# The second gate computed in the first gate's tile during the MLP, rings of five weight tiles, and a new table of order and engines

## The chip, the cores and the metric

The kernel runs on one core of a Trainium2 chip. The metric is device microseconds for one execution; the number for a kernel is the median of its runs. The engines are PE (matrix products), DVE (vector), ACT (scalar functions), POOL (GpSimd) and SP, which here only issues DMA transfers.

## The reference

One layer over 512 tokens of width 1024, one batch, all in fp32:

```
sh1, sc1, gt1, sh2, sc2, gt2 = split(silu(c) @ w_ada + b_ada, 6)
h = rms_norm(x) * (1 + sc1) + sh1
q, k, v, iq, ik, iw, ca, cg = split(h @ w_in)
attn = sparse attention: indexer scores (iq, ik, iw), top 128 keys a query
       (causal by chunks of 64), softmax over these, 8 heads of 64
conv = silu(layer_norm(depthwise conv of 31 taps (ca * sigmoid(cg))))
x = x + gt1 * (concat(rms_norm(attn), rms_norm(conv)) @ w_out)
h2 = rms_norm(x) * (1 + sc2) + sh2
out = x + gt2 * (relu(h2 @ w_ff1)^2 @ w_ff2)          # D_FF = 4096
```

`c` is one row of 1024, so each of the six parts of the first line is one row of 1024 that depends on no token. `gt1` scales the output projection, `gt2` the MLP's result at the very end.

## The kernel before

Every fp32 product is made of three products of split operands: a value is kept as a rounded part `hi` and a rest `lo = x - hi`, and `mm3` multiplies hi·hi, hi·lo and lo·hi into one PSUM bank. Weights are loaded raw (`wr_`, 512 KB a load), cast to `wh_` on ACT and subtracted to `wl_` on DVE or POOL (`split_now`, line 857). `wh_` and `wl_` come from rings of four tiles of 128x512 each: a fifth split waits until the first tile's last matmul has read it.

No engine's order is written out by hand. The code records every operation (`_Plan`, line 211), and `schedule` (line 308) walks through a model of the engines and starts, on each free engine, the ready operation of the lowest level. The levels come from the table `URG`, the engine of an operation that could run on several comes from `ENG` (P is POOL, V is DVE, A is ACT, T is PE), and `POOL_TAPS` says how many of the 31 convolution taps of each of four feature groups run on POOL. Where an entry of `ENG` has four letters, they stand for the four weight tiles of a group of loads or for the four parts of a matrix in turn. `issue` (line 402) then emits all instructions in that order from one line, so every row of the trace carries L436; tiles are told apart by name.

In order of time: loads and `ada` products (the six parts of the first line), input projections (`c`, `iq`, `q`, `k`, `v`), convolution taps (`run` on DVE, `cacc` on POOL), index scores and top-k (`m`, `sc`: eight maxima a step, MAX8 and MATCH_REPLACE8), attention for tokens 0 to 255 (`pS` scores, `sl` softmax, `pP` transposes, `pO`), the output projection (`oA` and `oC` into `x`), attention for tokens 256 to 511 (with `oB`), and the MLP. The MLP works through four blocks of 1024 of D_FF: block 0 for the first 256 tokens (`fA`, `yA`), blocks 1 to 3 for all 512 tokens (`fF`, then `ff2_seven`, line 1595), block 0 for the last 256 tokens (`fB`, `yB`). `ff2_seven` makes the second product from seven products of sums of quarters (p1, p7, p2, p6, p4, p5, p3, of 24 matmuls each) where the plain way would need eight: `t1F` and `qF` are sums of weight quarters, `fF` sums of activations, `wl_p1F` and so on the rests of those sums, `llp1F` the rests of activations, and `facc` and `uF` collect the results out of PSUM.

The two gates: `gt1` is computed on PE (`ps_gt`, then spread to all partitions). `gt2` is computed by `add_gemv_vector` (line 782): eight loads of 512 KB rows of `w_ada`, one multiplication and seven multiply-adds of 128x1024 on DVE into the tile, then the sum over partitions as two products with a matrix of ones (`pg_gt`) and two additions of the bias. Both gates have a tile of 128x1024 of their own; gt2 is recorded ahead of the MLP's first operation, with a level that puts it early in the program. It is first read in the last block (`finish`, line 1581).

Of the kernel before, what the change touches and what calls it, by code (L numbers as in the profile page):

```python
# [11 lines left out]
F32 = mybir.dt.float32  # L12
F32R = mybir.dt.float32r
# [17 lines left out]
NEG_MASK = -1.0e30  # L31
FILLER = False
URG = dict(
    ahead_c1=1128.32, ahead_iq=281.4, warm=-938.21, g0=-145.45, gr=-855.15, w72=-213.15, ps72=247.73,
    start=-1053.53, glu=-116.74, c0=-592.48, ik=-123.04, iq=-263.01, iqn=762.72, idx=-479.26, rel=-170.37,
    topk=183.27, c1=788.58, q=79.07, qn=394.99, k=113.44, kn=-88.5, qT=190.86, v=212.78, vn=-145.05, kT=-114.04,
    tapV0=3.46, tapV1=-1171.22, tapV2=354.3, tapV3=88.85, tapP0=89.85, tapP1=1138.33, tapP2=-785.21,
    tapP3=-939.21, sh2=46.69, sc2=777.66, gt1=-370.45, gt2=-144.05, gemv_step=20.799999999999997,
    ahead_x=550.67, ahead=102.55, cn=128.0, pyc=-1037.03, oC=476.28, attn=-1036.57, sm=-332.0999999999998,
    pv=-4.8000000000000345, sq=-97.20000000000007, oA=402.92, n2=50.33, ff=639.29, tapVs=27.400000000000006,  # L40
    tapPs=81.65000000000006, topks=9.050000000000011, idxs=12.400000000000002, ns=22.250000000000007,
    projs=6.549999999999992, cns=33.55000000000003, oCs=9.299999999999999, evict=403.92, usum=28.34,
    attns=33.15000000000006, topkB=1515.0, qTB=381.12, attnB=201.26, oB=693.93, n2B=653.09,
)
ENG = dict(
    sl0B="P", sl1B="V", oAmul0="P", oAmul1="P", oAadd0="P", oAadd1="P", oBmul0="P", oBmul1="P", oBadd0="V",
    oBadd1="V", gt1="T", gt2="V", round0="T", round1="T", round2="T", round3="T", sl0="A", sl1="P", rope_q="P",
    rope_k="P", rope_iq="P", gb="P", oAadd="P", oCmul="A", oAmul="V", lo_c0="V", lo_c1="V", lo_iq="P", lo_q="P",
    lo_k="P", lo_v="P", lo_oC="P", lo_oA="P", lo_oB="P", lo_f1A="PPVP", lo_f2A="PVPV", lo_f1F="PVVP",
    lo_f2F="VVPP", lo_f1B="VVVV", lo_f2B="VVVP", sumF="VPVV", losF="VVVV", fsumF="V", fhiF="A", floF="V",  # L50
    uaddF="V", foldF="V", frest="V", h2lo0="V", h2lo1="V", aff0="A", aff1="A", mixA="P", tap0="A",
)
POOL_TAPS = (7, 5, 11, 12)
NB = 4
NA = 1
NBLK = 16
# [460 lines left out]
def layer_kernel(  # L517
# [24 lines left out]
    pl = _Plan(tc)  # L542
# [27 lines left out]
    def blk(shape, dt, name):  # L570
        return big.tile(shape, dt, tag="B", bufs=NBLK, name=name)
# [9 lines left out]
    def wk_bank(name):  # L581
        return pwk.tile([P, 512], F32, tag="wk", name=name)
# [4 lines left out]
    def raw(ap):  # L587
        return ap.bitcast(F32)
# [125 lines left out]
    sh2 = const.tile([P, KD], F32, name="sh2")  # L714
# [136 lines left out]
    def split_weights(src, name, lo_eng, place=None):  # L851
        with pl.urgency(pl.level[0] - URG.get("ahead_" + name[:2], URG["ahead"])):
            return split_now(src, name, lo_eng, place)

    def split_now(src, name, lo_eng, place):
        r = wts.tile([P, 2, 512], F32, tag="raw", name=f"wr_{name}", fifo=True)
        if len(src.shape) == 4:
            for j in range(2):
                pl.sync.dma_start(r[:, j, :].rearrange("p (s c) -> p s c", s=2), src[:, j])
        else:  # L860
            pl.sync.dma_start(r, src)
        res = []
# [175 lines left out]
    rope_q = Rope(g_q, "q", HD**-0.5)  # L1038
# [59 lines left out]
    for ct in range(4):  # L1098
# [13 lines left out]
    for i in range(1, NT):  # L1112
        n = (i + 1) * P
        sc[i] = const.tile([P, n], F32, name=f"sc{i}")
        for h in range(H):
            pl.level = (URG["idx"] + (8 * i - 8 + h) * URG["idxs"],)
            ps = wk_bank(f"pidx{i}_{h}")
            q = slice(i * P, (i + 1) * P)
# [3 lines left out]
            rel = ps  # L1122
# [65 lines left out]
    qT = []  # L1188
# [3 lines left out]
    kT = [blk([P, 4, S], F32R, f"kT{a}") for a in range(2)]  # L1192
# [12 lines left out]
    for t in range(NT):  # L1205
        v = banks[t].rearrange("p (h d) -> p h d", d=HD)
# [386 lines left out]
    def ff2_seven(b, part, f, lev_load, start):  # L1595
# [7 lines left out]
        with pl.after([start]), pl.urgency(lev_load):  # L1603
            for g, n in ((0, 0), (0, 1), (1, 1), (1, 0)):
                q = blk([P, 4, 512], F32, f"q{part}{b}{g}{n}")
# [126 lines left out]
    for part, blocks in PHASES:  # L1732
        for b in blocks:
            fts = []
            pair = blk([P, 2, 4, 256], F32, f"f{part}{b}") if part in SEVEN and part != "F" else None
            mark = len(pl.ops)
            for g in range(2):
                step += 1
                pl.level = (URG["ff"] + 20 * step,)
                fts.append(ff1(b, g, part, pair))  # L1740
            start = next(op for op in pl.ops[mark:] if op.engine == "tensor")
            if part in SEVEN:
                lev_load = pl.level[0] - 20
                step += 1
                pl.level = (URG["ff"] + 20 * step,)
                step += 1
                ff2_seven(b, part, fts, lev_load, start)
                for h in dict(A=(0,), B=(1,), F=(0, 1))[part]:
                    count[h] += 1
                continue  # L1750
            for n in range(2):
                step += 1
                pl.level = (URG["ff"] + 20 * step,)
                ff2(b, n, part, fts)
            for h in dict(A=(0,), B=(1,), F=(0, 1))[part]:
                count[h] += 1
# [53 lines left out]
```

## Time and profile before

| | |
|---|---|
| median of 3 runs | 648.05 us (646.64 to 649.21) |
| profiled execution | 649.53 us |
| its span, first to last instruction | 647.4 us |
| mean granted clock of PE | 0.993 |
| busy: PE, DVE, ACT, POOL | 624.2, 512.1, 368.1, 285.1 us |
| HBM read | 89.73 MB |

The span is 2.1 us shorter than the profiled execution: what lies around the first and last instruction isn't in the trace. A busy time counts the engine's own instructions; matmuls overlap, so a duration of 0.39 us for a matmul of 128x512 says less than the distance from one to the next. The stage table further down cuts the span into the stages named above.

### The profile page before, as it was taken

The page shows a single profiled execution, that of the slowest core. Times are in us where ns is not written, and L with a number is a line of the kernel's source. Part 1 is how long each engine was busy: PE and PEld are TensorE (multiplying, and loading weights), DVE is VectorE, ACT ScalarE, POOL GpSimd, SP SyncE. Part 2 cuts the span into 40 slices and gives each one's busy share as a digit, 9 for nine tenths or more (in the row PEclk, how much of TensorE's full clock was granted, in tenths as well). Part 3 has the DMA queues.
Part 4 walks back from the last instruction along what each step waited for, and adds up shares of the span by engine and source line. Part 5 has one row for each costly group of instructions (what it writes and reads, how often), then busy time and mean ns, then how long its engine had stood idle before and what let it go on. Part 6 is the DMA issues. An engine that isn't in the chain of part 4 may idle for free.

```text
span 647.4 us, 9888 instructions
## 1 busy us (share of the span) xinstructions
PE 624.2 (96%) x3390; PEld 500.7 (77%) x3390; DVE 512.1 (79%) x998; ACT 368.1 (57%) x745; POOL 285.1 (44%) x291
## 2 busy tenths in 40 slices
PE   4999999999999899999999999999999999999997
PEld 3766687778776677789878888878887888878985
DVE  4657999999999899997484638985389953699975
ACT  3326534985539853997375438744485435765552
POOL 3007915999999687637573611025110151100011
PEclk9999999999999799999999999999999999999999
DMA  9969997523120162144727830029310183100772
GB/s 291 348 200 399 382 334 243 201 80 98 33 76 24 33 222 73 33 136 126 227 67 251 302 97 2 1 62 336 108 48 1 42 316 98 32 2 2 221 219 79
DMA packets 56219, 94.55 MB, mean 146 GB/s; under 512 B 5913, under 2 KB 22505, under 8 KB 56170
## 3 DMA queue, kind: packets, MB, share of 16 engines
q1 hardware_dynamic: 56074, 93.91, 43.9%
q8 instruction: 26, 0.43, 0.3%
q14 instruction: 23, 0.19, 0.1%
q10 hardware_dynamic: 96, 0.03, 0.0%
HBM read 89.73 MB, written 2.10 MB: 142 GB/s over the span
## 4 chain that ended last, share of the span: by engine, by line
PE 62%; DVE 14%; POOL 7%; ACT 5%; SPq 4%; issue 4%; DMA 3%; ACTq 0%; DVEq 0%; POOLq 0%
PE fF L436 20%; SPq L436 4%; PE c L436 4%; PE fB L436 4%; PE yB L436 3%; PE oC L436 3%; PE yA L436 3%; PE fA L436 3%; PE iq L436 3%; PE p5F L436 3%; PE p1F L436 2%; DVE sc L436 2%; PE p4F L436 2%; PE p3F L436 2%; DVE run L436 2%
## 5 line engine op out<-in xcount | busy, mean ns | idle before, releaser
L436 PE MATMUL fF<-h,wh_fF 128*128 128x512 f32 x384 | 118.3, 389 | 0.0
L436 PEld LDWEIGHTS fF<-h,wh_fF 128*128 128x128 f32 x384 | 72.1, 188 | 15.0
L436 POOL TENSOR_TENSOR wl_fF<-wr_fF,wh_fF 128x512 fp32r<-128x512 f32 x24 | 36.1, 1523 | 103.5 <-ACT wh_fF L436 63.5
L436 PE MATMUL fF<-h,wl_fF 128*128 128x512 f32 x192 | 74.8, 390 | 0.2 <-POOL wl_fF L436 0.2
L436 ACT CAST wh_fF<-wr_fF 128x512 fp32r<-128x512 f32 x48 | 29.5, 622 | 60.3 <-PE fF L436 41.2
L436 DVE SCALAR_TENSOR_TENSOR run<-u,wdw,run 128x512 f32<-128x512 f32 x85 | 60.4, 745 | 0.2
L436 PEld LDWEIGHTS fF<-h,wl_fF 128*128 128x128 f32 x192 | 36.0, 188 | 8.0 <-POOL wl_fF L436 0.6
L436 POOL TENSOR_TENSOR cacc<-cacc,prod 128x512 f32<-128x512 f32 x31 | 40.0, 1292 | 4.7 <-ACT prod L436 3.4
L436 POOL TENSOR_TENSOR wl_yB<-wr_yB,wh_yB 128x512 fp32r<-128x512 f32 x4 | 5.1, 1288 | 69.6 <-ACT wh_yB L436 69.6
L436 ACT ACTIVATE fF<-fF 128x512 f32<-128x512 f32 x48 | 29.1, 613 | 7.2 <-PE fF L436 5.8
L436 DVE TENSOR_TENSOR wl_p1F<-qF,wh_p1F 128x512 fp32r<-128x512 f32 x12 | 8.3, 689 | 28.4 <-PE fF L436 28.4
L436 POOL TENSOR_TENSOR qF<-qF,qF 128x512 f32<-128x512 f32 x9 | 14.0, 1552 | 37.0 <-issue 22.0
L436 DVE TENSOR_TENSOR qF<-qF,qF 128x512 f32<-128x512 f32 x27 | 26.1, 992 | 1.4 <-DMA qF<-in_w_ff_dram 1.1
L436 POOL TENSOR_TENSOR wl_iq<-wr_iq,wh_iq 128x512 fp32r<-128x512 f32 x8 | 10.2, 1290 | 38.6 <-ACT wh_iq L436 38.6
L436 PE MATMUL c<-hTlo,wh_c 128*128 128x512 f32 x64 | 25.9, 405 | 0.2 <-DVE hTlo L436 0.2
L436 DVE TENSOR_TENSOR wl_fF<-wr_fF,wh_fF 128x512 fp32r<-128x512 f32 x24 | 16.7, 710 | 11.7 <-ACT wh_fF L436 11.4
L436 DVE MATCH_REPLACE8 sc<-m,sc 128x256 f32<-128x256 f32 (+2 forms) x48 | 25.7, 539 | 0.0
L436 PE MATMUL c<-hThi,wl_c 128*128 128x512 f32 x64 | 25.4, 397 | 0.0
L436 DVE MAX8 m<-sc 128x8 f32<-128x256 f32 (+2 forms) x48 | 25.1, 545 | 0.0
L436 PE MATMUL c<-hThi,wh_c 128*128 128x512 f32 x64 | 24.4, 401 | 0.7 <-ACT hThi L436 0.6
L436 ACT ACTIVATE prod<-u,wdw 128x512 f32<-128x512 f32 x31 | 21.9, 719 | 4.0 <-POOL cacc L436 3.9
L436 PE MATMUL fA<-h2a,wh_fA 128*128 128x256 f32 x128 | 23.9, 286 | 0.0
(394 smaller groups left out, 1972.7 us busy)
## 6 DMA issues: line engine op xcount, KB each, us to landing
wr_fF<-in_w_ff_dram SPq DMA_DIRECT2D x24, 512.0 KB, 3.8
qF<-in_w_ff_dram SPq DMA_DIRECT2D x24, 512.0 KB, 9.2
wa_gt<-in_w_ada_dram SPq DMA_DIRECT2D x16, 512.0 KB, 9.0
ada<-in_w_ada_dram SPq DMA_DIRECT2D x12, 512.0 KB, 8.7
wr_c<-in_w_in_dram SPq DMA_DIRECT2D x16, 256.0 KB, 7.6
wa_sh<-in_w_ada_dram SPq DMA_DIRECT2D x8, 512.0 KB, 7.6
wa_sc<-in_w_ada_dram SPq DMA_DIRECT2D x8, 512.0 KB, 6.8
wr_fA<-in_w_ff_dram SPq DMA_DIRECT2D x8, 512.0 KB, 3.9
```

Source lines behind the costliest of these rows:

```text
L436: f(*map(real, args), **{k: real(v) for k, v in kwargs.items()})
```

## The change

`gt2` has no tile of its own any more: it is `gt1`'s tile, written again. Its loads and its arithmetic are recorded in the first MLP block, after that block's first matmul, and can begin to write once `gt1` has been read for the last time. The place that its tile took (4 KB a partition) goes to the rings of `wh_` and `wl_`, which have five tiles each. The tables of levels and engines are new throughout: the rows further down show what stands where.

```diff
 URG = dict(... all levels new, among them:
-    ... gt1=-370.45, gt2=-144.05, ... pyc=-1037.03, attn=-1036.57, evict=403.92, topkB=1515.0, ...
+    ... gt1=-76.15, gt2=738.68, ... pyc=1384.16, attn=62.53, evict=-5.0, topkB=1218.7, ...
 ENG = dict(...
-    sl1B="V", oBmul1="P", oBadd1="V", lo_f1A="PPVP", lo_f2A="PVPV", lo_f2F="VVPP",
-    lo_f1B="VVVV", lo_f2B="VVVP", sumF="VPVV", losF="VVVV",
+    sl1B="P", oBmul1="V", oBadd1="P", lo_f1A="PVPP", lo_f2A="VPVV", lo_f2F="VVPV",
+    lo_f1B="VVPP", lo_f2B="VPVV", sumF="VVVV", losF="VVVP",
-POOL_TAPS = (7, 5, 11, 12)
+POOL_TAPS = (9, 5, 11, 10)
@@ in split_now and, with the same two lines, in right (ff2_seven)
-                hi = wts.tile([P, 512], F32R, tag="whi", name=f"wh_{name}{j}", fifo=True)
-                lo = wts.tile([P, 512], F32R, tag="wlo", name=f"wl_{name}{j}", fifo=True)
+                hi = wts.tile([P, 512], F32R, tag="whi", bufs=5, name=f"wh_{name}{j}", fifo=True)
+                lo = wts.tile([P, 512], F32R, tag="wlo", bufs=5, name=f"wl_{name}{j}", fifo=True)
@@
-    gt2 = const.tile([P, D], F32, name="gt2")
+    gt2 = gt1
@@ ahead of the MLP's loop
-    gate("gt2", 5 * D, gt2)
@@ in the loop over the MLP's blocks
             start = next(op for op in pl.ops[mark:] if op.engine == "tensor")
+            if step == 2:
+                with pl.after([start]):
+                    gate("gt2", 5 * D, gt2)
```

`sl1B` is the softmax scaling of the second half's second tile; `lo_f1A`, `lo_f2A`, `lo_f1B`, `lo_f2B` say who makes `wl_fA`, `wl_yA`, `wl_fB`, `wl_yB`; `sumF` the four sums of weight quarters (`t1F`, `qF`) and `losF` the four `wl_p` of a product. `lo_f2F` isn't used, since blocks F go through `ff2_seven`. `evict` is how much earlier than its product's successors the reading of a PSUM bank is placed.

What that moves at three places. First PE where the first half's attention begins. Before, the products of `sc2` (`ps_sc`) and three groups of `py` (transposes of the convolution) stand well ahead of it, among the matmuls of `v`:

```order
L436 MATMUL v_1954<-wh_v_1891,hThi_293 128x512
L436 MATMUL ps_sc_1981<-wa_sc_1167,c_144 32x256 x8
L436 MATMUL ps_sc_1981<-wa_sc_1246,c_144 32x256 x8
L436 MATMUL ps_sc_1981<-wa_sc_1273,c_144 32x256 x8
L436 MATMUL py_2016<-ident,cacc 128x128 x4
L436 MATMUL py_2027<-ident,cacc 128x128 x4
L436 MATMUL py_2036<-ident,cacc 128x128 x4
L436 MATMUL v_1902<-wl_v_2013,hThi_293 128x512
L436 MATMUL v_1902<-wh_v_1891,hTlo_309 128x512
L436 MATMUL v_1902<-wh_v_1907,hThi_293 128x512
L436 MATMUL v_1919<-wl_v_2013,hThi_293 128x512
```

Now `ps_sc` and half of `py` stand behind the first scores (`pS`), and the last matmuls of `v` ahead of them:

```order
L436 MATMUL v_1883<-wh_v_1970,hTlo_472 128x512
L436 MATMUL pS_0_0_2165<-kT_2053,qT_2155 128x256
L436 MATMUL pS_0_1_2168<-kT_2053,qT_2155 128x256
L436 MATMUL pS_0_0_2165<-kT_2059,qT_2155 128x256
L436 MATMUL pS_0_1_2168<-kT_2059,qT_2155 128x256
L436 MATMUL pS_0_0_2165<-kT_2053,qT_2155 128x256
L436 MATMUL pS_0_1_2168<-kT_2053,qT_2155 128x256
L436 MATMUL py_2184<-ident,cacc 128x128 x4
L436 MATMUL ps_sc_2197<-wa_sc_978,c_144 32x256 x8
L436 MATMUL pS_1_0_2217<-kT_2053,qT_2155 128x256
L436 MATMUL pS_1_1_2219<-kT_2053,qT_2155 128x256
```

The four groups of ps_sc and two groups of py moved behind the first pS; of v, none follows the first pS now, where nine matmuls did.

Second, DVE and gate 2. Before, its multiply-adds stand between the convolution's taps (`run`), early in the program:

```order
L436 SCALAR_TENSOR_TENSOR run_684<-u,wdw,run_684 128x512
L436 TENSOR_TENSOR rlo_gt_959<-ps_gt_700,rhi_gt_946 128x256
L436 SCALAR_TENSOR_TENSOR run_684<-u,wdw,run_684 128x512
L436 SCALAR_TENSOR_TENSOR gt_890<-wa_gt_802,cth,gt_890 128x1024
L436 SCALAR_TENSOR_TENSOR run_684<-u,wdw,run_684 128x512
L436 SCALAR_TENSOR_TENSOR gt_890<-wa_gt_818,cth,gt_890 128x1024
L436 SCALAR_TENSOR_TENSOR run_684<-u,wdw,run_684 128x512
L436 COPY ik_tok<-pt_991 128x4x64
L436 SCALAR_TENSOR_TENSOR run_684<-u,wdw,run_684 128x512
```

Now they stand in the first MLP block, behind the last reading of `gt1` (`x<-x,gt`) and among the splits of `wl_yA` and the transposed activations `h`:

```order
L436 SCALAR_TENSOR_TENSOR x_2905<-oB_3_3911,rA_3641,x_2905 128x512
L436 TENSOR_TENSOR x_2905<-x_2905,gt_1924 128x512 x2
L436 TENSOR_SCALAR gt_1924<-wa_gt_3341,cth 128x1024
L436 TENSOR_SCALAR xn_3933<-x_2905,rstd_3946 128x1024
L436 TENSOR_TENSOR wl_yA_3977<-wr_yA_3758,wh_yA_3958 128x512
L436 TENSOR_TENSOR wl_yA_3999<-wr_yA_3792,wh_yA_3964 128x512
L436 TENSOR_TENSOR wl_yA_4007<-wr_yA_3792,wh_yA_3979 128x512
L436 CAST h_3316<-ht_3994 128x4x128
L436 TENSOR_TENSOR wl_yA_4020<-wr_yA_3822,wh_yA_3987 128x512
L436 TENSOR_TENSOR h_3357<-ht_3994,h_3316 128x4x128
L436 CAST h_3568<-ht_4012 128x4x128
L436 SCALAR_TENSOR_TENSOR gt_1924<-wa_gt_3341,cth,gt_1924 128x1024
```

All ten DVE instructions of gate 2 moved, the first three of 128x1024 to the first MLP block, five more to the beginning of the first F block, and the two bias additions ahead of the last block.

Third, DVE in an F block, here product p4 of the third of them (`qF` sums, `llp4F` and `wl_p4F` rests, `uF<-p6F` readings of PSUM). Before:

```order
L436 TENSOR_TENSOR qF_5626<-qF_5649,qF_5609 128x512 x2
L436 TENSOR_TENSOR llp4F_6145<-fF_5917,lhp4F_6111 128x512
L436 TENSOR_TENSOR wl_p4F_6154<-qF_5626,wh_p4F_6125 128x512
L436 TENSOR_TENSOR uF_0_5996<-p6F_0_6087,uF_0_5996 128x512
L436 TENSOR_TENSOR uF_1_6007<-p6F_1_6115,uF_1_6007 128x512
L436 TENSOR_TENSOR llp4F_6170<-fF_5917,lhp4F_6147 128x512
L436 TENSOR_TENSOR wl_p4F_6176<-qF_5626,wh_p4F_6138 128x512
L436 TENSOR_TENSOR wl_p4F_6181<-qF_5626,wh_p4F_6151 128x512
L436 TENSOR_TENSOR wl_p4F_6185<-qF_5626,wh_p4F_6163 128x512
```

Now:

```order
L436 TENSOR_TENSOR qF_5618<-qF_5644,qF_5609 128x512
L436 TENSOR_TENSOR llp4F_6127<-fF_5915,lhp4F_6111 128x512
L436 TENSOR_TENSOR wl_p4F_6132<-qF_5618,wh_p4F_6116 128x512
L436 TENSOR_TENSOR wl_p4F_6139<-qF_5618,wh_p4F_6125 128x512
L436 TENSOR_TENSOR llp4F_6145<-fF_5915,lhp4F_6136 128x512
L436 TENSOR_TENSOR wl_p4F_6150<-qF_5618,wh_p4F_6142 128x512
L436 TENSOR_TENSOR fF_5752<-fF_5752,fF_5915 128x2x256
L436 TENSOR_TENSOR uF_0_5993<-p6F_0_6109,uF_0_5993 128x512
L436 TENSOR_TENSOR uF_1_6006<-p6F_1_6118,uF_1_6006 128x512
```

One of four wl_p4F has gone to POOL, and the two readings of p6F, which stood among the first of them, now stand behind the three that are left. On POOL the end of that block, before (the `wl_fF` are the next stage's weights, the `qF` sums of quarters):

```order
L436 TENSOR_TENSOR wl_fF_5750<-wr_fF_5614,wh_fF_5742 128x512
L436 TENSOR_TENSOR wl_fF_5869<-wr_fF_5725,wh_fF_5864 128x512
L436 TENSOR_TENSOR wl_fF_5879<-wr_fF_5725,wh_fF_5871 128x512
L436 TENSOR_TENSOR qF_5609<-qF_5609,qF_5626 128x512
L436 TENSOR_TENSOR qF_5626<-qF_5649,qF_5609 128x512
L436 TENSOR_TENSOR wl_yB_6693<-wr_yB_6586,wh_yB_6688 128x512
```

And now:

```order
L436 TENSOR_TENSOR wl_fF_5866<-wr_fF_5714,wh_fF_5861 128x512
L436 TENSOR_TENSOR wl_p1F_5945<-qF_5609,wh_p1F_5938 128x512
L436 TENSOR_TENSOR wl_p7F_5995<-qF_5618,wh_p7F_5987 128x512
L436 TENSOR_TENSOR wl_p2F_6051<-qF_5644,wh_p2F_6045 128x512
L436 TENSOR_TENSOR wl_p6F_6105<-qF_5609,wh_p6F_6098 128x512
L436 TENSOR_TENSOR wl_p4F_6159<-qF_5618,wh_p4F_6153 128x512
L436 TENSOR_TENSOR wl_p5F_6213<-t1F_5675,wh_p5F_6207 128x512
L436 TENSOR_TENSOR wl_p3F_6267<-qF_5630,wh_p3F_6260 128x512
L436 TENSOR_TENSOR wl_fB_6334<-wr_fB_5841,wh_fB_6323 128x512
```

POOL has one split of each of the seven products and none of the sums.

## Rows read from the trace of the kernel before

**Rows 1.** The page, engines over the span: busy us, share, instructions.
```profile
PE 624.2 (96%) x3390; PEld 500.7 (77%) x3390; DVE 512.1 (79%) x998; ACT 368.1 (57%) x745; POOL 285.1 (44%) x291
```

**Rows 2.** Busy us of each engine by stretch, with clock and DMA share.
```profile
core 0: us, PE busy (x) PEld busy (x) DVE busy (x) ACT busy (x) POOL busy (x), PEclk, DMA share, GB/s
110.00:170.00 60.00, 59.51 (x319) 46.40 (x317) 58.89 (x118) 44.93 (x86) 56.58 (x54) 1.00 0.39 123
170.00:196.00 26.00, 25.39 (x173) 19.03 (x173) 25.72 (x64) 9.53 (x17) 25.10 (x39) 1.00 0.19 61
196.00:234.00 38.00, 34.48 (x182) 25.41 (x183) 34.45 (x118) 33.93 (x112) 31.46 (x42) 0.91 0.15 50
234.00:262.00 28.00, 28.00 (x122) 21.41 (x120) 27.90 (x66) 9.87 (x17) 21.65 (x19) 1.00 0.39 122
262.00:295.00 33.00, 32.02 (x219) 25.80 (x219) 31.56 (x88) 29.75 (x84) 13.02 (x18) 1.00 0.32 98
295.00:350.00 55.00, 54.14 (x319) 47.54 (x318) 35.65 (x46) 34.17 (x77) 35.82 (x32) 1.00 0.49 153
475.00:515.00 40.00, 39.58 (x172) 31.70 (x171) 39.60 (x65) 25.86 (x46) 4.53 (x3) 1.00 0.00 1
598.00:621.00 23.00, 23.00 (x192) 22.95 (x191) 22.43 (x40) 12.85 (x26) 0.00 (x0) 1.00 0.74 219
```

**Rows 3.** The chain that ended last: start us, us, engine, output.
```profile
105.47 0.86 PE pg_gt L436 x2
...
349.62 43.52 PE fF L436 x192
393.14 5.44 PE p1F L436 x24
...
597.69 23.03 PE fB L436 x192
```

**Rows 4.** All instructions that write tile gt: count, ns min/median/max, first and last start.
```profile
L436 DVE SCALAR_TENSOR_TENSOR gt<-wa_gt,cth,gt x7: 1275/1276/2059, 80.3 to 98.7; 128x1024 f32<-128x1024 f32 x7
L436 DVE TENSOR_TENSOR gt<-pg_gt,wa_gt x2: 691/692/692, 106.4 to 108.8; 128x512 f32<-128x512 f32 x2
L436 DVE TENSOR_SCALAR gt<-wa_gt,cth x1: 1258/1258/1258, 73.8 to 73.8; 128x1024 f32<-128x1024 f32 x1
```

**Rows 5.** PE in order of time, 172 to 200: start us, us, instruction.
```profile
173.98 2.80 PE L436 MATMUL ps_sc<-wa_sc,c 128*32 128x256 f32 x48
176.71 1.53 PE L436 MATMUL py<-ident,cacc 128*128 128x128 f32 x12
...
180.94 1.07 PE L436 MATMUL ps_sc<-wa_sc,c 128*32 128x256 f32 x16
...
195.92 0.61 PE L436 MATMUL pS<-kT,qT 64*128 64x256 f32 x3
```

**Rows 6.** DVE's instructions by shape, 196 to 262: count, busy us, mean ns.
```profile
L436 DVE SCALAR_TENSOR_TENSOR mixC<-pyc,hgoc,mixC 128x512 fp32r<-128x512 f32 x4 | 3.0, 739 | 0.0
```

**Rows 7.** Tile sl, its scalings on DVE.
```profile
L436 DVE TENSOR_SCALAR sl<-sl,rl x8: 410/472/1574, 265.1 to 288.2; 128x384 f32<-128x384 f32 x4, 128x512 f32<-128x512 f32 x4
```

**Rows 8.** DVE in order of time, 562 to 570.
```profile
563.20 0.68 DVE L436 TENSOR_TENSOR fF<-fF,fF 128x512 f32<-128x512 f32 x1
563.80 0.68 DVE L436 TENSOR_TENSOR facc<-p1F,facc 128x512 f32<-128x512 f32 x1
```

**Rows 9.** DVE in order of time, 355 to 372.
```profile
362.62 5.12 DVE L436 TENSOR_TENSOR qF<-qF,qF 128x512 f32<-128x512 f32 x3
```

**Rows 10.** POOL in order of time, 355 to 372.
```profile
360.36 3.44 POOL L436 TENSOR_TENSOR wl_fF<-wr_fF,wh_fF 128x512 fp32r<-128x512 f32 x2
```

**Rows 11.** POOL in order of time, 560 to 570.
```profile
563.41 1.63 POOL L436 TENSOR_TENSOR qF<-qF,qF 128x512 f32<-128x512 f32 x1 [7.32 <-issue]
```

**Rows 12.** Tile wl_fB on DVE.
```profile
L436 DVE TENSOR_TENSOR wl_fB<-wr_fB,wh_fB x16: 674/677/685, 596.2 to 616.4; 128x512 fp32r<-128x512 f32 x16
```

**Rows 13.** DVE in order of time, 255 to 267: the second half's first softmax step.
```profile
261.73 0.54 DVE L436 CUSTOM_DVE_ANT_0 sl<-pS,sc 128x384 f32<-128x384 f32 x1
```

More of the change, by code (lines that the diff above doesn't have):

```diff
@@ L33 @@
 URG = dict(
[L34 to L43, printed above, removed]
+    ahead_c1=785.07, ahead_iq=32.760000000000005, warm=123.78, g0=-1833.06, gr=-14.88, w72=-113.68, ps72=-29.24,
@@ new lines @@
+    start=-1746.81, glu=154.06, c0=-1187.39, ik=-36.16, iq=-1121.33, iqn=-16.44, idx=-496.69, rel=647.01,
+    topk=-1760.95, c1=334.2, q=-176.53, qn=781.53, k=3.36, kn=-356.64, qT=-22.47, v=153.45, vn=704.82, kT=14.09,
+    tapV0=-342.43, tapV1=-1268.03, tapV2=382.11, tapV3=179.6, tapP0=-306.72, tapP1=764.66, tapP2=-468.72,
+    tapP3=-1348.42, sh2=53.45, sc2=251.02, gt1=-76.15, gt2=738.68, gemv_step=26.599999999999998, ahead_x=607.75,
+    ahead=31.76, cn=197.5, pyc=1384.16, oC=354.55, attn=62.53, sm=-341.49999999999994, pv=65.39999999999996,
@@ L44 @@
+    sq=-88.80000000000005, oA=324.82, n2=406.58, ff=618.75, tapVs=32.25, tapPs=82.10000000000002,
+    topks=29.650000000000006, idxs=13.749999999999996, ns=2.399999999999989, projs=14.149999999999999,
+    cns=24.70000000000005, oCs=7.449999999999996, evict=-5.0, usum=13.149999999999999, attns=22.750000000000103,
+    topkB=1218.7, qTB=-1665.33, attnB=391.42, oB=663.89, n2B=104.61,
 )
 ENG = dict(
-    sl0B="P", sl1B="V", oAmul0="P", oAmul1="P", oAadd0="P", oAadd1="P", oBmul0="P", oBmul1="P", oBadd0="V",
@@ L47 @@
-    oBadd1="V", gt1="T", gt2="V", round0="T", round1="T", round2="T", round3="T", sl0="A", sl1="P", rope_q="P",
+    sl0B="P", sl1B="P", oAmul0="P", oAmul1="P", oAadd0="P", oAadd1="P", oBmul0="P", oBmul1="V", oBadd0="V",
+    oBadd1="P", gt1="T", gt2="V", round0="T", round1="T", round2="T", round3="T", sl0="A", sl1="P", rope_q="P",
     rope_k="P", rope_iq="P", gb="P", oAadd="P", oCmul="A", oAmul="V", lo_c0="V", lo_c1="V", lo_iq="P", lo_q="P",
-    lo_k="P", lo_v="P", lo_oC="P", lo_oA="P", lo_oB="P", lo_f1A="PPVP", lo_f2A="PVPV", lo_f1F="PVVP",
@@ L50 @@
-    lo_f2F="VVPP", lo_f1B="VVVV", lo_f2B="VVVP", sumF="VPVV", losF="VVVV", fsumF="V", fhiF="A", floF="V",
+    lo_k="P", lo_v="P", lo_oC="P", lo_oA="P", lo_oB="P", lo_f1A="PVPP", lo_f2A="VPVV", lo_f1F="PVVP",
+    lo_f2F="VVPV", lo_f1B="VVPP", lo_f2B="VPVV", sumF="VVVV", losF="VVVP", fsumF="V", fhiF="A", floF="V",
     uaddF="V", foldF="V", frest="V", h2lo0="V", h2lo1="V", aff0="A", aff1="A", mixA="P", tap0="A",
 )
-POOL_TAPS = (7, 5, 11, 12)
+POOL_TAPS = (9, 5, 11, 10)
 NB = 4
@@ L1637, in right @@
         def right(src, k, name):
-            hi = wts.tile([P, 512], F32R, tag="whi", name=f"wh_{name}{k}", fifo=True)
-            lo = wts.tile([P, 512], F32R, tag="wlo", name=f"wl_{name}{k}", fifo=True)
+            hi = wts.tile([P, 512], F32R, tag="whi", bufs=5, name=f"wh_{name}{k}", fifo=True)
+            lo = wts.tile([P, 512], F32R, tag="wlo", bufs=5, name=f"wl_{name}{k}", fifo=True)
             pl.scalar.copy(hi, src[:, k, :])
```

## The prediction

> **What bounds the kernel now.** I began with the page's first part: PE is busy for 96% of the span, DVE for 79%, ACT and POOL for far less [rows 1]. A busy PE is not proof, so I next took busy times by stage, and the chain of waits beside it. From 110 to 196 us (projections, index scores, convolution taps) PE and DVE are both full: 59.51 and 58.89 of 60 us, then 25.39 and 25.72 of 26. In the first half's attention, 196 to 234, both leave about 3.5 us of 38 idle, and the granted clock averages 0.91: a part of it ran at the lower level of 1.2 GHz. From 234 to 262 PE (28.00 of 28) and DVE (27.90) are full again. In the second half's attention, 262 to 295, ACT has 29.75 of 33. In the MLP's first block DVE has 35.65 of 55, so there is room [rows 2].
>
> For the three long F blocks the chain is the better view: 192 matmuls take 43.52 us and a product's 24 take 5.44, both 0.2267 us each [rows 3]. A block of 192 and seven products is thus 81.6 us at that pitch, three are 244.8, and the trace has 597.69 - 349.62 = 248.07 [rows 3]. All that could be won in F is 3.3 us. DVE is gapless in the products of the second block (39.60 of 40.00 us [rows 2]), so it is DVE that costs these 3.3 us, and what slows DVE there goes straight to the end. The last f stage is full on PE (23.00 of 23 [rows 2]).
>
> The profiled run took 649.53 us, 2.1 more than its span and 1.5 more than the median of 648.05. The sum goes from 649.53; at the end 1.5 comes off. The measurement can tell about 0.5%, 3.2 us, from no change.
>
> **The change, part by part.**
>
> *Gate 2 leaves the front.* DVE loses 10.1 (seven), 1.26 and 1.38 (two of 0.69), 12.7 us between 73 and 109; PE loses two visits of two matmuls, 0.86 us each on the chain: 1.7 us [rows 3, 4]. Nothing there needs gate 2.
>
> *What PE does before the attention.* By the order of the instructions the ps_sc products (2.80 + 1.07 us) and two of the four py groups (8 of 12 in 1.53 us: 1.0) now stand behind the first pS; against that no v matmul stands behind it now, where nine did (9 x 0.227 = 2.0) [rows 3, 5]. PE reaches its first pS earlier by 1.7 + 3.9 + 1.0 - 2.0 = 4.6 us. DVE, by the same order, has less to do before its first softmax too: gate 2's ten instructions (12.7 us by durations, 10.3 from start to start, since neighbours overlap) and some small ones (1.6) are gone, five top-k steps of 0.6 have come, 8.9 in all. So it doesn't hold PE back. Term: -4.6, between 0 and -8.9.
>
> *Attention of half 0.* PE receives 4.9 us and gives 2.0. The stage has 3.5 us of idle PE and a stretch at the lower clock [rows 2]; ps_sc and py wait for nothing and can go into the holes between pS and pP. DVE loses four mixC (0.74 each [rows 6]), three smaller qT and three top-k rounds, and gains a few from the stage ahead: about 5.5 us less. If PE were the path, +2.9; if DVE were, -4. I take -1, since neither engine is full here.
>
> *Between the halves.* The mixC and qT come back here on DVE: +4.1 us by the order. But DVE enters with 8.9 + 5.5 less to do, so its net lead is 10.3 us, more than PE's. PE's 28.00 stay: 0, at most +4.
>
> *Attention of half 1.* Eight scalings of sl go from DVE (0.47 each, 3.8 us [rows 7]) to POOL, which has 13.02 of 33 us; ACT, nearly full, keeps its work. -1, between -4 and 0.
>
> *First MLP block.* Gate 2's 12.7 us, four more wl_yA and two x<-x,gt come to DVE, part of it before F begins: 5.5 us here against 19 us of room [rows 2]. Its loads, nine of 512 KB or 4.7 MB, come too: the stretch runs at 153 GB/s with a DMA share of 0.49, so they are about 15 us of a queue that is free for 28. They wait for the first matmul of the block, and gt's first write waits for the last x<-x,gt; nothing is queued behind on SP but weights of the same block and the next. If that cover were gone, all of 12.7 us. I take +1.
>
> *F blocks.* Per block three qF and one t1F come from POOL to DVE, one split (wl) of each product goes from DVE to POOL, and the evictions come later on DVE. Net five instructions fewer a block; neighbours start 0.60 us apart (563.20, 563.80 [rows 8]), so 3.0 us less DVE in a block. What it costs depends on one thing. Three qF on DVE took 5.12 us, 1.71 each, while POOL split weights from 360.36 on [rows 9, 10]; a DVE instruction of that shape elsewhere takes 0.68 [rows 8]. One POOL split beside gapless DVE can thus cost 1.03 us. But the POOL qF at 563.41 cost nothing: beside it DVE ran facc<-p1F, which reads PSUM, in 0.68 [rows 8, 11]. The new splits are the fourth of each product, and two PSUM evictions stand close to them on DVE. I take three of seven blocked, 3.1 against 3.0, and the rest of the gain in the earlier wl_p4F: -1 over all blocks; bounds -3.3 (all of the excess) and +12.6 (all seven blocked: 7 x 1.03 - 3.0 = 4.2 a block).
> The Trainium skill, page "SBUF — State Buffer", section "Who interferes with whom", says that a DVE instruction with two SBUF inputs contends with a GpSimd instruction that reads SBUF, and that the loser waits for the whole instruction. The 1.71 beside the 0.68 agrees, and the free run beside a PSUM eviction does too. The rule speaks against this part of the change: by it every split that meets qF, fF or wl on DVE costs, which leads to the slower rival below.
>
> *Last block.* Gate 2's two PE visits now stand before fB: +1.7, PE is full there. DVE loses eight wl_fB (5.4 us [rows 12]) and gains two gt additions; it isn't the bound: 0.
>
> *The rings of five.* They would tell where a cast waits for a free tile. Where F waits, DVE is gapless instead: 0.
>
> Sum: -4.6 - 1 + 0 - 1 + 1 - 1 + 1.7 = -4.9. That is 644.6 on the profiled run and 643.1 against the median. Its own range, with attention 0 and F a few us off either way, is 638 to 646.5.
>
> **Rivals.**
>
> *The front is paid back in the attention (no change).* The ps_sc and py matmuls aren't hidden but stand between pS and pP: +2.9 instead of -1, and F gives nothing. Then -4.6 + 2.9 - 1 + 1 + 0 + 1.7 = 0: 648. For it: PE's idle of 3.5 us is less than the 4.9 that come. Against it: nothing waits for ps_sc and py, and the granted clock of 0.91 tells that PE's work isn't dense there.
>
> *DVE was the bound all along (a larger gain).* DVE is as full as PE from 110 to 196 and 234 to 262 [rows 2]. If it is DVE that PE follows, the second softmax starts 10.3 us earlier: -10.3 - 1 + 1 - 1 + 1.7 = -9.6, 638.4. Against it: PE has its own work in all these stages, only 1.7 us less.
>
> *The shared port (slower).* POOL's splits block DVE in the products. It decides from the third of seven blocked splits on, where 3.1 us eat the 3.0 won. At five, 5 x 1.03 - 3.0 = 2.15 a block, 6.5 over three; with the -3.9 of the other terms +2.6, 650.6. At seven 12.6 - 3.9 = +8.7, 656.8, and eight wl_fB on POOL may add up to 2.8. For it: DVE has 0.4 us of slack in 40 there. Against it: the evictions beside it, and the 0.68 there [rows 8]. I put it at 652.
>
> *The loads come in the way.* SP issues gate 2's rows ahead of some wr_fA and wr_yA. If MLP weights wait behind half of the 15 us, +7.5 where +1 was taken: 649.6. For it: both are on one queue. Against it: the free share of 0.51.
>
> **How the numbers follow.** The forecast has 0.45, the front paid back 0.19, the larger gain 0.13, the port 0.18, the loads 0.05. Faster by over 0.5% (below 644.8) takes 0.31 of the forecast's 0.45 (its centre lies 1.7 us inside that bound), the larger gain (0.13) and 0.04 of the rest: 0.48. Slower by over 0.5% (above 651.3) takes three quarters of the port's chance and 0.03 of the others: 0.16. Within 0.5%: 0.36. The range reaches below to the middle of the larger gain's case, less 1.4 for its spread, and above to the port's case at five to six splits: 637 to 652.
>
> **What would show it.** First pS near 191 instead of 195.92; second softmax 4 to 7 us earlier than 261.73 [rows 13]. The gt rows on DVE between 315 and 365, with no wait on PE for them; wr_fA and wr_yA without a late landing. In F, DVE qF, fF and wl that last 1.3 us or more beside a POOL wl would show the port; all at 0.68 would show it harmless; three blocks that take under 247 us would show F's gain. I am wrong if the first pS comes earlier but the second softmax doesn't (front paid back), if fF to fB grows beyond 249 us (port), or if fA waits on its weights (loads).

## The result, and the profile after

The changed kernel takes 656.51 us (median of 5, 652.92 to 656.74), the kernel before in the same job 649.21: ratio 1.0109, 95% interval 1.0089 to 1.0130. It is slower by 1.1% where 643.1 was forecast, and lies outside the range of 637 to 652. A second job with the same kernel gave 655.52 and 1.011 (1.0079 to 1.0140). The profiled execution took 652.92 us, the least of the five, so a second one was taken too ("again" below, 654.96 us).

Start of the first matmul of each stage, from the two traces and that of before (us; in brackets against before):

| | before | after | again |
|---|---|---|---|
| pS, first half's attention | 195.92 | 190.59 (-5.3) | 190.61 (-5.3) |
| fF, first F block | 349.46 | 343.36 (-6.1) | 341.59 (-7.9) |
| fF, third F block | 514.60 | 507.60 (-7.0) | 507.87 (-6.7) |
| p1F, third F block | 558.12 | 555.95 (-2.2) | 554.80 (-3.3) |
| fB, last block | 597.53 | 596.38 (-1.2) | 597.31 (-0.2) |
| yB | 620.56 | 624.79 (+4.2) | 626.84 (+6.3) |

So the front is won nearly as forecast, and lost again in two places in both traces: the first stage of the third F block (4.8 and 3.4 us) and the last block's fB (5.4 and 6.5). In the second trace the products lose more: from p1F to the last matmul of p3F the three blocks take 37.9, 38.9 and 38.9 us in the first trace, 37.9, 40.9 and 41.0 in the second, and took 38.0, 39.2 and 39.2 before. The page, answering [rows 1]: PE and DVE are busy as before, POOL has 44 us more.

```profile
PE 622.3 (96%) x3390; PEld 501.3 (77%) x3390; DVE 511.5 (79%) x977; ACT 370.0 (57%) x745; POOL 329.3 (51%) x312
```

Busy time by stretch of after, answering [rows 2]; the columns are those there, the stretches moved with the stages. The attention of the first half still has the clock of 0.91, the first MLP block still has room on DVE (38.48 of 53.40). The last row is fB: PE, full there before, is busy for 19.75 of 23.00 us, at a mean clock of 0.93.

```profile
190.60:230.00 39.40, 35.89 (x243) 24.21 (x242) 35.47 (x120) 33.91 (x111) 33.37 (x47) 0.91 0.13 42
...
290.00:343.40 53.40, 52.89 (x311) 46.65 (x312) 38.48 (x49) 32.00 (x72) 29.71 (x25) 1.00 0.66 207
...
596.40:619.40 23.00, 19.75 (x150) 19.31 (x149) 16.39 (x23) 8.92 (x18) 14.73 (x7) 0.93 0.57 174
```

The first pS of after on PE's timeline, where [rows 5] had 195.92:

```profile
190.59 0.65 PE L436 MATMUL pS<-kT,qT 64*128 64x256 f32 x6
```

And on DVE's timeline the first softmax step of the second half, where [rows 13] had 261.73. They are 5.3 and 5.2 us earlier.

```profile
256.51 0.54 DVE L436 CUSTOM_DVE_ANT_0 sl<-pS,sc 128x384 f32<-128x384 f32 x1
```

Gate 2 in its new place, answering [rows 4]: the seven multiply-adds last 1.28 us each as before and stand at 329 to 351. The bias additions, ahead of the last block by the order of DVE, run at 598.7 and 599.3, when fB's matmuls have already begun (596.38).

```profile
L436 DVE SCALAR_TENSOR_TENSOR gt<-wa_gt,cth,gt x7: 1271/1275/1285, 329.2 to 351.3; 128x1024 f32<-128x1024 f32 x7
L436 DVE TENSOR_TENSOR gt<-pg_gt,wa_gt x2: 675/676/678, 598.7 to 599.3; 128x512 f32<-128x512 f32 x2
L436 DVE TENSOR_SCALAR gt<-wa_gt,cth x1: 752/752/752, 322.0 to 322.0; 128x1024 f32<-128x1024 f32 x1
```

The chain that ended last, answering [rows 3]. It goes through POOL twice: for a wl_fF at 508.82 and for one wl_fB that took 6.42 us, where a POOL subtraction of this shape takes 1.29. In the products it goes through DVE as well, for a wl_p6F at 574.02.

```profile
508.82 2.99 POOL wl_fF L436
511.85 44.26 PE fF L436 x187
...
574.02 0.69 DVE wl_p6F L436
...
595.22 1.72 PE pg_gt L436 x4
596.94 2.52 PE fB L436 x21
...
600.07 6.42 POOL wl_fB L436
...
606.53 18.42 PE fB L436 x139
624.96 20.44 PE yB L436 x90
```

That wl_p6F came late because DVE's llp6F ahead of it took 1.78 us instead of 0.68, beside POOL's wl_p6F at 571.81 (1.74 us); PE waited 0.66 us for it. The second block has the same wait at 487.3.

```profile
572.32 1.78 DVE L436 TENSOR_TENSOR llp6F<-fF,lhp6F 128x512 fp32r<-128x512 f32 x1
```

What DVE did while that wl_fB waited, in order of time (start, us, instruction): instruction after instruction with both inputs in SBUF, 0.60 us apart and each 0.68 long, undisturbed. The last of them ends at 605.36; POOL's ends at 606.49, 1.13 us later. The second trace has the same hold, 6.53 us.

```profile
599.87 1.28 DVE L436 TENSOR_TENSOR facc<-facc,gt 128x512 f32<-128x512 f32 x2
601.07 1.28 DVE L436 TENSOR_TENSOR facc<-facc,x 128x512 f32<-128x512 f32 x2
602.27 1.28 DVE L436 TENSOR_TENSOR facc<-facc,gt 128x512 f32<-128x512 f32 x2
603.48 1.28 DVE L436 TENSOR_TENSOR x<-x,facc 128x512 f32<-128x512 f32 x2
604.68 0.68 DVE L436 TENSOR_TENSOR wl_fB<-wr_fB,wh_fB 128x512 fp32r<-128x512 f32 x1
```

After each of the two waits PE in this trace ran at the lower of its two levels, 1.2 GHz, for some 3 us: busy times by stretch right behind the waits that ended at 511.85 and 606.53, the granted clock in the third column from the right. The waits themselves are 2.00 us (behind one of 0.66) and 3.25; 187 matmuls of fF then take 44.26 us. In the second trace PE waits at the same place for 0.81 and 2.02 us, the granted clock stays at 1.00, and the same 187 take 42.68; so the lower clock costs another 1.6 here, and doesn't follow each time. In that trace's fB, behind a wait of 3.36 us, PE runs at it for over 5 us.

```profile
511.80:513.80 2.00, 1.95 (x5) 1.56 (x6) 0.00 (x0) 0.00 (x0) 0.00 (x1) 0.50 0.40 58
513.80:516.00 2.20, 2.20 (x8) 1.77 (x7) 0.00 (x0) 0.00 (x0) 0.00 (x0) 0.68 0.94 345
606.50:608.00 1.50, 1.47 (x10) 1.47 (x11) 0.00 (x0) 0.00 (x0) 1.50 (x2) 0.79 0.30 37
608.00:610.00 2.00, 2.00 (x11) 2.00 (x11) 0.00 (x0) 0.45 (x1) 0.97 (x1) 0.50 0.84 225
```

### The profile page after: what moved, and what is told of

It reads as the page before. It is cut to its first block, busy times and chain, and to the rows that moved or that the text cites. A ratio compares the mean times of both kernels' runs of the same rounds, so it can differ in the third digit from the quotient of the medians.

```text
span 651.1 us, 9908 instructions
## 1 busy us (share of the span) xinstructions
PE 622.3 (96%) x3390; PEld 501.3 (77%) x3390; DVE 511.5 (79%) x977; ACT 370.0 (57%) x745; POOL 329.3 (51%) x312
## 5 line engine op out<-in xcount | busy, mean ns | idle before, releaser
L436 POOL TENSOR_TENSOR wl_fF<-wr_fF,wh_fF 128x512 fp32r<-128x512 f32 x24 | 38.1, 1596 | 83.6 <-DVE wl_fF L436 30.9
L436 DVE TENSOR_TENSOR qF<-qF,qF 128x512 f32<-128x512 f32 x36 | 31.7, 906 | 1.1 <-DMA qF<-in_w_ff_dram 0.6
L436 DVE TENSOR_TENSOR wl_fF<-wr_fF,wh_fF 128x512 fp32r<-128x512 f32 x24 | 18.4, 794 | 13.8 <-ACT wh_fF L436 13.4
L436 PE MATMUL fB<-h,wh_fB 128*128 128x256 f32 x128 | 24.9, 297 | 0.0
L436 POOL TENSOR_TENSOR wl_fB<-wr_fB,wh_fB 128x512 fp32r<-128x512 f32 x8 | 16.9, 2134 | 11.6 <-ACT wh_fB L436 11.6
```

The source lines that it names most:

```text
L436: f(*map(real, args), **{k: real(v) for k, v in kwargs.items()})
```

## The experiments

Theory S: POOL's subtractions, the new wl_p and wl_fB, are held up while DVE runs two-input instructions from SBUF without a gap, and PE waits for the held one. Each run's order is planned anew from its tables, so an edit of engines moves other instructions too; where that matters it is said. All times are medians; "before" in the same jobs was 648.3 to 648.8.

**The changed kernel once more.** No edit.

> The changed kernel once more, unaltered. Its profiled execution (652.92 us) was 3.6 us faster than the median of its own runs (656.51), so one trace does not show all. Theory S (POOL's subtractions are held up for as long as DVE runs instruction after instruction with two SBUF inputs): the slower executions show one more or one longer hold of a POOL wl_ in fF, in a product or in fB, 3 to 4 us; ratio to before 1.009 to 1.013. Rival F (the front differs from run to run, loads or attention): the slower executions reach the first F block later, and F is as long as in the first trace (253.0 us from fF0 to fB).

Measured: 655.52 us, 651.92 to 659.46 over six executions. Both theories have something: the front differs by 1.8 us between the two traces, and F with fB by 3.8 (fF to yB 281.4 and 285.3; before 271.1). But the longer F doesn't come of one more hold on POOL, as S had it: it comes of DVE giving way more often. The same product, p4 of the second F block, shows it. In the first trace POOL's timeline has a wl_p4F that is held for 3.48 us:

```profile
490.93 3.48 POOL L436 TENSOR_TENSOR wl_p4F<-qF,wh_p4F 128x512 fp32r<-128x512 f32 x1 [4.84 <-ACT wh_p4F L436]
```

DVE's timeline there goes on undisturbed, 0.68 an instruction:

```profile
490.16 1.28 DVE L436 TENSOR_TENSOR wl_p4F<-qF,wh_p4F 128x512 fp32r<-128x512 f32 x2
491.36 0.68 DVE L436 TENSOR_TENSOR llp4F<-fF,lhp4F 128x512 fp32r<-128x512 f32 x1
...
493.17 1.28 DVE L436 TENSOR_TENSOR uF<-p6F,uF 128x512 f32<-128x512 f32 x2
```

(POOL's ended at 494.40, 1.23 us after DVE's uF<-p6F at 493.17 began, which reads PSUM.) In the second trace, at the same place, POOL's timeline has the same instruction done in 1.67 us:

```profile
489.15 1.67 POOL L436 TENSOR_TENSOR wl_p4F<-qF,wh_p4F 128x512 fp32r<-128x512 f32 x1 [4.84 <-ACT wh_p4F L436]
```

and DVE's has the llp4F beside it, which takes 1.78 instead of 0.68:

```profile
488.39 1.28 DVE L436 TENSOR_TENSOR wl_p4F<-qF,wh_p4F 128x512 fp32r<-128x512 f32 x2
489.60 1.78 DVE L436 TENSOR_TENSOR llp4F<-fF,lhp4F 128x512 fp32r<-128x512 f32 x1
```

One program, one place, either outcome, and POOL's instruction begins 0.16 us after DVE's second wl_p4F in both. Of the 21 wl_p on POOL nine last 2.2 to 3.5 us in the first trace, and five last 2.2 to 2.4 in the second; five make a DVE instruction last about 1.78 in the first and nine in the second. Where DVE gives way in p6 or p5, PE waits 0.6 to 0.66 us each time, and the second trace's two products stages of 40.9 and 41.0 us are those with four such places instead of two. That fits the spread of 652 to 659, which two traces can't show.

**fB's splits back on DVE.**

```diff
-lo_f1B="VVPP"
+lo_f1B="VVVV"
```

> The changed kernel with lo_f1B back to VVVV: all 16 wl_fB on DVE, nothing else edited. Theory S: the hold of 6.42 us on POOL at 600.07 and PE's wait of 3.4 us behind it are gone; fB takes about 23.0 us again instead of 28.3 and the time falls by 3.4 to 5 us against the changed kernel (ratio to before 1.002 to 1.006). Rival G (gate 2's additions on DVE right before the last block hold it up): those stay, fB stays near 28 us and the ratio stays 1.009 to 1.013.

Measured: 650.73 us, ratio 1.0024 (1.0001 to 1.0047), 4.8 us less than the changed kernel. fB to yB takes 23.4 us where the changed kernel had 28.4, with gate 2's additions still at their place (600.5, fB from 597.6 on): S, not G. F from fF to fB stays long, 255.7 us.

**The products' fourth split back on DVE.**

```diff
-losF="VVVP"
+losF="VVVV"
```

> The changed kernel with losF back to VVVV: the fourth wl_p of each product on DVE, not POOL; the sums qF stay on DVE, which so has 71 + 7 instructions in a block's products. Theory S: POOL is free when the wl_fF of the next F block are cast, the two that were held for 6.61 us at 505.19 start 2 us earlier, and 2 to 4 us of the 4.8 us lost at the start of the last F stage come back; DVE's seven instructions more (4.2 us a block) cost 0 to 1.5 us a block in the products. Ratio 1.003 to 1.012. Rival P (DVE is what the splits on POOL slow down): DVE instructions in the products that lasted over 1 us go back to 0.68 and the products' stages get shorter by 2 us a block; ratio under 1.000.

Measured: 647.71 us, ratio 0.9988 (0.9973 to 1.0003), 7.8 us less than the changed kernel: more than S had said, and a ratio just under 1.000, where P had put it. So the run shows what these splits on POOL cost, not which engine pays; by the two traces above both do. From the first fF to the first fB PE waits nowhere for over 0.3 us; the stage takes 243.8 us (fB's first matmuls stand among the last of p3F). What is left of the loss is fB, where PE is busy for 27.4 us of the 31.0 from 590 to 621. No wl_fB on POOL is held there, the longest of the eight takes 1.74 us. PE's three waits of 1.27, 0.73 and 1.62 us end with a wl_fB on DVE, and DVE's last up to 1.78 us. The first of these waits stands also in the run below with all wl_fB on DVE; in the others it is DVE that pays.

**All three entries back.**

```diff
-lo_f1B="VVPP", sumF="VVVV", losF="VVVP"
+lo_f1B="VVVV", sumF="VPVV", losF="VVVV"
```

> The changed kernel with lo_f1B, losF and sumF as before the change: the engines of the F blocks and of wl_fB as in the kernel before, gate 2 and all levels as changed. Theory S: the loss of 4.8 at the last F stage and of 3.4 in fB goes, the front's gain of 6 us stays, gate 2's products before fB cost 1.7: 644 to 646 us on the scale where before is 649.2, ratio 0.992 to 0.997. Rival O (the loss is due to the new order on DVE, evictions late, not to POOL): F stays 4 us longer than before, ratio 0.998 to 1.004. Rival F: ratio near 1.005.

Measured: 643.25 us, ratio 0.9915 (0.9901 to 0.9930): the front's gain without the loss, and faster than both kernels. Its executions lie within 1.3 us (642.70 to 644.02). F falls by the ratio. O isn't excluded by this run, though the levels of the change are all there: with the engines the order on DVE went back too. The readings of p6F stand behind the first wl_p4F as in the kernel before (and early in the other runs without wl_p on POOL), and gate 2's products run at 491 and 501 instead of 595. What speaks against O is PE's waits: in both traces of the changed kernel each one of over 0.3 us in F ends with a wl_fF on POOL or with a wl_p on DVE behind an instruction of 1.78 us, none with a reading of PSUM. A run with late readings and no split on POOL wasn't made. In the long stages the chain of this kernel goes along PE, and fF's 192 matmuls of the second block take 43.53 us, where [rows 3] has 43.52. POOL's two wl_fF ahead of the third block are held here as well, 7.35 us for two, but from 502.56 on and not from 505.19, and PE waits only 0.6 us for them:

```profile
424.23 43.53 PE fF L436 x192
...
509.96 42.68 PE fF L436 x187
...
593.54 22.07 PE fB L436 x184
```

**Only the sums left on DVE.**

```diff
-lo_f1B="VVPP", losF="VVVP"
+lo_f1B="VVVV", losF="VVVV"
```

> The changed kernel with lo_f1B and losF on DVE as before, but the sums qF and t1F left on DVE (sumF VVVV). Of the three entries of the table that concern POOL in F and fB this leaves one changed. Theory S: no POOL split in the products or in fB is left, DVE has four instructions more per block than in the run with all three undone (2.4 us of 81): 643 to 646, ratio 0.992 to 0.997. Rival P (DVE is full in the products, so the sums are dear there): 2.4 us more in each of three blocks, ratio 1.000 to 1.004.

Measured: 643.70 us, ratio 0.9926 (0.9910 to 0.9942). The sums cost 0.45 us, which is not to be told from nothing. With this run the losses add up: wl_fB on POOL costs 4.8 (with the products' splits there) or 4.0 (without), the products' splits on POOL cost 7.8 or 7.0; both together 11.8, and 12.3 with the sums.

**POOL's splits kept, DVE's run broken up.** If S is right, it should help to leave the engines alone and only move DVE's instructions away.

```diff
                 if number(t) == NB - 1 and not more:
-                    finish(t, n)
+                    later.append((finish, t, n))
                 if number(t) == NB - 2 and not more and t // 2 not in seven_last and n == 1:
-                    fold(t, n)
+                    later.append((fold, t, n))
...
+                mid = len(pl.ops)
                 fts.append(ff1(b, g, part, pair))
+            if part == "B":
+                with pl.after([next(op for op in pl.ops[mid:] if op.engine == "tensor")]):
+                    for f, t, n in later:
+                        f(t, n)
```

> The changed kernel, with the eight multiplications and additions of finish and the four of fold that follow the last F block put behind the first matmul of fB's second group (recorded later, with that matmul ahead of them). All engines stay as changed: eight wl_fB on POOL, the fourth wl_p of each product on POOL. Theory S: POOL's subtraction that was held for 6.4 us beside eight such DVE instructions gets through in at most 3 us, PE doesn't wait 3.4 us for it, and the time falls by 3 to 5 us against the changed kernel: ratio to before 1.003 to 1.007. Rival W (POOL is simply too slow for wl_fB at 1.29 us a piece, twice DVE's 0.60, whatever DVE does): the ratio stays 1.009 to 1.013 and PE waits for POOL's wl_fB elsewhere in fB.

Measured: 650.89 us, ratio 1.0024 (1.0000 to 1.0047), 4.6 us less than the changed kernel's 655.52, with the same eight wl_fB on POOL. The row of these eight (ns, least, median and most) in the changed kernel:

```profile
L436 POOL TENSOR_TENSOR wl_fB<-wr_fB,wh_fB x8: 1274/1479/6415, 596.0 to 619.5; 128x512 fp32r<-128x512 f32 x8
```

and the same row of this one: the 6.4 us are gone, the rest is as it was. From fB to yB it takes 23.4 us in the profiled execution, at 646.46 us the fastest of the twelve, and PE waits for nothing in fB. F's loss is still there, 253 us from fF to fB. W falls.

```profile
L436 POOL TENSOR_TENSOR wl_fB<-wr_fB,wh_fB x8: 1293/1400/2108, 593.8 to 612.4; 128x512 fp32r<-128x512 f32 x8
```

**Gate 2 moved alone.** First by the kernel's own means: the change's lines on gt2 in the kernel before, with gate 2's new level.

> The kernel before with gate 2 alone moved: gt2 is gt1's tile and is recorded behind the first matmul of the first MLP block, with the level it has in the change; tables, taps and rings of four as before. By the prediction's steps PE loses 1.7 us ahead of the attention and gets it back before fB, and the 4.6 us come from what the new table moves: first F block 1.5 to 3 us earlier than 349.5, ratio 0.996 to 1.001. Rival D (DVE was the bound of the front, and its 12.7 us of gate 2 the whole gain): first F block 6 to 8 us earlier, ratio 0.990 to 0.994.

Measured: 690.61 us, ratio 1.0651 (1.0631 to 1.0671). Neither theory: the levels of before, without gate 2's work in front, give another order, and the first pS comes at 222.6. It says nothing of gate 2. The second attempt held the order of all other instructions as in before and put only gate 2's elsewhere (the plan is made with gate 2 in front, its operations are taken out and put in later).

> The kernel before with gate 2 alone moved, and this time the order of everything else held as before word for word: gate 2's eight instructions of 128x1024 go on DVE from the first MLP block on, four pairs some eight DVE instructions apart, its loads one pair ahead, its sums over partitions ahead of the last block; gt2 is gt1's tile, rings of four. By the prediction's steps PE alone matters in front: first pS 1.7 us earlier, first F block 1.7 to 3 us earlier, 1.7 back before fB, ratio 0.997 to 1.002. Rival D (DVE was the bound of the front): first F block 6 us or more earlier, ratio under 0.994. DVE has 8 instructions of 1.3 us more around the first F block, where it has room.

Measured: 649.86 us, ratio 1.0023 (1.0010 to 1.0036). First pS 1.3 us earlier, first F block 3.5 earlier; 0.9 is given back in the first F block and 2.4 in the last products ahead of fB. Rival D falls. The steps of the prediction hold roughly: 1.3 where 1.7 was forecast, 3.5 where 1.7 to 3, 2.4 where 1.7. Gate 2's move alone is worth nothing at the end; of the 6 to 8 us in front it makes about half, the rest of the change (order, engines, taps, rings) the other.

**Rings of four.** The kernel with all three entries back, with four tiles a ring.

```diff
-tag="whi", bufs=5   ...   tag="wlo", bufs=5
+tag="whi", bufs=4   ...   tag="wlo", bufs=4
```

> The run with lo_f1B, losF and sumF as before, now with rings of four instead of five; the plan moves with it from the start on. By the prediction the rings are worth nothing: ratio as with five, 0.990 to 0.994. Rival R (the fifth tile lets casts and splits run ahead): casts wait for a free tile, the splits come later, ratio 0.995 or more, with waits of PE in fF or in the products where there were none.

Measured: 669.32 us, ratio 1.0332 (1.0311 to 1.0354). The first pS comes at 206.5, 15 us later than with five. As in gate_only the plan went elsewhere, so this shows that the table, tuned for five tiles, is bad with four, and not what a fifth tile is worth under a fixed order, which wasn't tried.

**The port by itself.** DVE and POOL alone, 128x512 as in the kernel.

> Not the layer: DVE runs rows of twelve 128x512 instructions without a wait, and two POOL subtractions of 128x512 with two SBUF inputs are released by the second of them; only that is computed, and parts of x copied out. Rows: A, twelve DVE additions with two SBUF inputs; B, the same with the seventh reading PSUM; C, from the second on all read PSUM; D, from the second on all multiply one SBUF input by a number; E, POOL has the port first, six subtractions against eight DVE additions. Theory S: in A the first POOL subtraction ends only after the twelfth DVE addition, 6 to 7.5 us long; in B it ends 1.2 us after the seventh starts, 3 to 4 us; in C both take 1.3; in E POOL keeps turns with DVE and DVE's additions take 1.3 to 1.8. Rival T (the two take turns whenever both want the port): A as E, POOL's subtraction under 2 us in every row, DVE's additions 1.3 us and more. D: either way not said by a run so far.

Measured, POOL's timeline:

```profile
5.87 1.64 POOL L577 TENSOR_TENSOR pA<-dA,a 128x512 f32<-128x512 f32 x1 [5.43 <-DVE dA L570]
7.48 1.71 POOL L579 TENSOR_TENSOR pA<-a 128x512 f32<-128x512 f32 x1
...
24.97 1.26 POOL L577 TENSOR_TENSOR pC<-dC,a 128x512 f32<-128x512 f32 x1 [6.23 <-DVE dC L572]
...
32.08 1.37 POOL L577 TENSOR_TENSOR pD<-dD,a 128x512 f32<-128x512 f32 x1 [4.63 <-DVE dD L574]
```

and DVE's, in groups of eleven instructions:

```profile
5.11 8.84 DVE L570 TENSOR_TENSOR dA<-a 128x512 f32<-128x512 f32 x11
...
24.21 6.66 DVE L572 TENSOR_TENSOR dC<-bank,a 128x512 f32<-128x512 f32 x11
...
31.59 5.91 DVE L574 TENSOR_SCALAR dD<-a 128x512 f32<-128x512 f32 x11
```

Beside PSUM reads (pC, dC) neither engine is slowed: 1.26 us for POOL, eleven in 6.66 for DVE. Beside two-input additions (pA, dA) the two take turns: POOL 1.64 and 1.71, eleven of DVE's in 8.84. Beside a multiplication of one SBUF input (pD, dD) they do too: POOL 1.37 and 1.44, two of DVE's 1.49 and 1.48 instead of 0.42. Row B has POOL at 1.64 again, where S had 3 to 4, and in row E they take turns as both theories had it. So S's expectation of a hold in rows A and B was wrong, and T's turns were right here. That POOL can be passed over eight times, as at 600.07, the small kernel doesn't reproduce. What decides between turns and a hold stays open; that both happen at one place of one program is shown above. So S is shown for the wl_fB of the last block, by the run with DVE's instructions moved away; in the products both engines pay.

## Why the prediction was wrong

*Gate 2 leaves the front; PE before the attention.* Right: 5.3 us where 4.6 were forecast, at the instruction named. *Attention of half 0 and between the halves:* -1 forecast, -0.5 and -2.5 in the two traces (first pS to last oC). *Attention of half 1 and first MLP block:* -1 and +1 forecast; from the last oC to the first fF it took 87.8 us before and 87.6 and 87.8 after, so the cover for gate 2's DVE work and its 4.7 MB was there. The front's sum, -5.6, met -6.1 and -7.9. That it came so near is in part luck: gate 2's move alone, under the old order, made 1.3 of the 5.3 us and 3.5 of the 6.1 to 7.9. *Last block, PE's two visits:* 1.72 us at 595.22, right. *The rings of five:* no run tests the 0.

*F blocks* failed. The step weighed only what DVE loses, 1.03 us a blocked split, against five instructions saved a block. The five were three: seven wl_p leave DVE in a block, three qF and one t1F come (120 such instructions in F before, 111 after), 1.8 us and not 3.0. Of the 21 splits five made DVE wait in the first trace and nine in the second, where nine were forecast. What was left out is the other side, POOL as the one that waits: nine of its 21 wl_p last 2.2 to 3.5 us in the first trace, its wl_p3F ends at 505.23, POOL comes late to the wl_fF of the next stage (from 505.19 on, two in 6.61 us), PE waits 2.7 us for these, and in the first trace then runs at half clock. In the first trace the products are no longer than before, and this stage alone takes 4.8 us more; in the second the products of two blocks add 1.7 us each as well. From fF to fB F took 253.0 and 255.7 us where 248.8 were forecast (248.07 - 1 + 1.7).

*Last block, wl_fB* failed likewise: "it isn't the bound: 0" looked at DVE alone, which has room there (16.39 of 23.00 us). The eight splits weren't priced on the engine they moved to, at the place where DVE has the finish instructions: one held for 6.42 us, 28.4 us from fB to yB instead of 23.0.

A row of the chain of before had shown it, and the prediction left it out: two wl_fF on POOL that took 4.71 us, where two alone take 2.6.

```profile
427.88 4.71 POOL wl_fF L436 x2
```

The rival on the shared port, at 0.18, had the right place and nearly the size (650.6 at five, 656.8 at seven, and 2.8 more for wl_fB), but the same one-sided price. Its signs came in part: fF to fB grew beyond 249 us, and five or nine DVE instructions in the products last 1.78; but at 490.93 DVE's last 0.68 while POOL waits. The Trainium skill, page "SBUF — State Buffer", section "Who interferes with whom", says that the loser blocks fully and that the order of issue decides who that is. The full blocking agrees with both traces (3.48 us on POOL, 1.78 on DVE); read with both engines as possible losers it would have named POOL's side, though not the size of a hold beside eight DVE instructions. That the order of issue decides isn't borne out where the same program has it either way, with POOL's start 0.16 us behind DVE's in both.

## What to carry to other kernels

When work moves from a full engine to an idle one and the two slow each other, as DVE and POOL do here, price it on both: what the full engine loses if it gives way, and how long the idle one is held if it doesn't, and look which of its results the bounding engine waits for next. A piece whose consumer comes 2 us later doesn't belong on the engine that was held for 6; beside DVE additions that read PSUM neither was slowed (row C). And a table of levels tuned for one program is good for that program: moving one operation cost 6.5% here and taking one buffer away 4%, so test a part by holding the order of the rest.

## What the runs showed of the hardware

A POOL subtraction was passed over by eight DVE instructions in a row (6.42 us for 1.29), yet in the small kernel the two engines take turns; both outcomes occur at one place of one program, with the same start to start distance. The kernel with POOL's splits in products and fB spreads over 7.5 us in six executions, the one without them over 1.3 in six; but the kernel before, also without them, spreads over 3.3 in 23, so the spread fits the contention and doesn't prove it. A wait of PE of 2.0 us in a stage that was otherwise full was followed by some 3 us at a granted clock of 0.50 in one execution and by none in another; behind waits of 3.25 and 3.36 us PE ran at 0.50 for some 3 and for over 5 us.
